# The gates' scratch layout in DRAM: by single first keys, or by groups of four

## The chip, the cores and the metric

One core of a Trainium2 chip runs the whole program. The metric is device time in microseconds (us) of one execution, the median over three runs. PE is the matrix engine and PEld its weight load, DVE the vector engine, ACT the scalar engine, POOL the general engine, SP the engine that only issues transfers. A "q" behind a name (SPq, ACTq) marks an instruction of that engine's sequencer, here the issue of a transfer.

## The reference

A transformer block over 512 tokens of width 1024: two attention mixers, an output projection, and then a PEER layer, which is what the change touches. Cut to its core:

```
q = (hf @ w_q).reshape(T, 8, 2, 128)
scores = einsum('thpd,hpnd->thpn', q, sub_keys)     # two key sets of 128 for each of 8 heads
s, idx = top_k(scores, 16)
cand = s[:, :, 0, :, None] + s[:, :, 1, None, :]    # 16 x 16 pairs
best, pos = top_k(cand, 16)
expert = take(idx0 * 128 + idx1, pos)               # 16384 experts: first key x second key
gate = softmax(best)
y[t] = sum over the 8 * 16 chosen: gelu(hf[t] . u[expert]) * gate * v[expert]
```

## The kernel before

Of the 512 tokens, 128 are served by gathering the rows of u and v that they chose (an indirect transfer on POOL's queue, line 1019, and two DVE passes over each gathered row; spread over the whole second half of the program). The other 384 are computed densely: for each of the 128 first keys e, PE multiplies the 128 experts (e, second key) with all 384 tokens ("up"), ACT applies Gelu, DVE multiplies the result with the gates of these experts (`weigh`), most of them zero, and PE multiplies it with v's 128 rows of e and adds into PSUM over all e ("down"). Matrices are split into a high and a low part (whi and wlo, vhi and vlo, chi and clo), ACT making the high and DVE the low one, and each product is three matmuls.

The gates must therefore be brought into a dense form: a tile of 128 second keys (partitions) by 384 tokens for every first key. That is done in two stages with a scratch tensor `gd` in DRAM between them.

**Writing stage, about 636 to 932 us.** Eight tokens at a time, `onehot` (DVE) makes one-hot matrices of the first and the second key, `spread` (PE, then ACT into `gs`) multiplies them, and when 32 tokens are together one transfer, issued by ACT (line 1191), writes `gs` (128 second keys x 128 first keys x 32 tokens, 2 MB) to `gd`. There are 12 such blocks; the last is written in 4 parts of 512 KB. `gs` has two buffers. Meanwhile `fill` lets PE do "up" products: `some` takes them a 24th at a time, `split_hi` (ACT, line 236) and `split_lo` (DVE) split u's matrix, `up_out` applies Gelu (ACT, line 964) and writes the result to `gad` by a transfer that ACT issues too (line 966). The order of instructions on each engine is fixed when the program is written: an engine runs its list in order, and issuing a transfer is an instruction in that list.

**Reading stage, about 940 to 1615 us.** For each first key in the order `order`: `down(n)`, and behind it on the other engines the work for keys two to four ahead. Keys come in groups of EG = 4; `g_load` (line 1288) reads one group's gates, 128 second keys x 12 blocks x 4 keys x 32 tokens, 768 KB, into `gt` (two buffers), as soon as `weigh` has used up the group two before. 30 of the 32 loads are issued by SP, the first two by POOL. SP's queue also carries v's rows (`vraw`, line 1269), the kept results (`ga`, read from `gad`, line 1316) and u's matrices (`raw`, line 223), in the order in which the program names them.

In `gd` before, one partition's row holds, for each block of 32 tokens, 128 first keys x 32 tokens. A write is 128 runs of 16 KB (in the last block 4 KB), a read of four keys is 128 x 12 runs of 4 x 32 x 4 bytes = 512 B.

Of the kernel before, what the change touches and what calls it, by code (L numbers as in the profile page):

```python
# [10 lines left out]
F32 = mybir.dt.float32  # L11
# [12 lines left out]
T = 512  # L24
# [27 lines left out]
GT = 128  # L52
# [141 lines left out]
def body(ctx, tc, a, out):  # L194
    nc = tc.nc
    pe, act, dve, pool, sp = (Metered(nc.tensor, _pe_ns), nc.scalar, Metered(nc.vector, _dve_ns), nc.gpsimd, nc.sync)
    ctx.enter_context(tc.manual_schedule())
    sb = ctx.enter_context(tc.tile_pool(name="sb", bufs=1))
    dr = ctx.enter_context(tc.tile_pool(name="dr", bufs=1, space=DRAM))
# [11 lines left out]
    queue, raws, ready = [], {}, {}  # L211
# [103 lines left out]
    def pmm(name="pmm"):  # L315
        return ps.tile([128, T], F32, name=name, bufs=4 if name == "pmm" else 2)
# [5 lines left out]
    def tmp(dt=F32, n=T):  # L322
        return tp[0].tile([128, n], dt, name="tmp", bufs=tp[1])
# [80 lines left out]
    def proj(key, xs=None, bank="pmm"):  # L404
        w = weights(key)
        p = pmm(bank)
        acc(p if key[0] != "u" else p[:, GT:], pairs(w, NC_D), xs or hx)
        if key[0] != "u":
            further(key)
        return p  # L410
# [74 lines left out]
    for c in range(NC_D):  # L485
# [28 lines left out]
        if c >= 3 and c - 3 < NT:  # L514
            tt = c - 3
            p = pmm("pst")
# [18 lines left out]
    for i in range(2):  # L535
        p = proj(("w1", 6 + i))
# [14 lines left out]
    for i in range(4):  # L551
        p = proj(("w1", 8 + i))
        t = tmp()
# [68 lines left out]
    for g in range(3):  # L622
        w = weights(("wq", g))
        for i in range(2):
            p = pmm()
# [9 lines left out]
            else:  # L635

                t, x = tmp(), tmp()
# [7 lines left out]
    for i in range(4):  # L645
        p = pmm()
# [5 lines left out]
        if i % 2 == 0:  # L652
            x = turned[i // 2]
# [7 lines left out]
    for tt in range(NT):  # L661
        ts = slice(tt * 128, (tt + 1) * 128)
        p = pmm()
# [142 lines left out]
    for mt in range(8):  # L806
        g = []
        for s in range(2):
            i = 2 * mt + s
            if i in EARLY:  # L810
                t = gin.pop(i)
            else:
                p = proj(("w1", 12 + i))
                t = tmp()
# [6 lines left out]
        for s, y in ((1, yb), (0, ya)):  # L821
            p = pmm()
# [11 lines left out]
    for mt in range(8):  # L834
        p = proj(("wo", mt), mgx)
# [132 lines left out]
    for mt in range(16):  # L968
# [3 lines left out]
        p = proj(("wpq", mt), h2x)  # L972
# [77 lines left out]
    NS = PH * TOPK  # L1050
    i1T, i2T, gh, gl = [pr.tile([128, ND], F16, name=n) for n in ("i1T", "i2T", "gh", "gl")]
    TB = 32
    gd = dr.tile([128, T // TB, 128, TB], F32, name="gd")
    GS = 2.0 ** 15
    def route(tt):
        s4 = srt[:, tt].rearrange("p (h s) k -> p h s k", s=2)
# [115 lines left out]
    def spread(o):  # L1172

        tb, k = divmod(o, SPT)
        if k == 0:
            gst[tb] = pr.tile([128, 128, TB], F32, name="gs", bufs=2)
        gs = gst[tb]
        e1, eh, el = hot.pop(o)
        for q in range(2):
            p = ps.tile([128, 4, 128], F32, name="pst" if q else "pk", bufs=2)  # L1180
            for i in range(4):
                g, t = 2 * q + i // 2, i % 2
                pe.matmul(p[:, i], eh[:, g, :, t], e1[:, g, :, t], start=True, stop=False)
                pe.matmul(p[:, i], el[:, g, :, t], e1[:, g, :, t], start=False, stop=True)
            act.activation(gs[:, :, 8 * k + 4 * q:8 * k + 4 * q + 4], p.rearrange("p t i -> p i t"), AF.Copy,
                           scale=1.0 / GS)
        if k == SPT - 1:
            parts = 4 if tb == T // TB - 1 else 1
            n = 128 // parts
            for i in range(parts):  # L1190
                act.dma_start(gd[:, tb, i * n:(i + 1) * n].rearrange("p i t -> p (i t)"),
                              gs[:, i * n:(i + 1) * n].rearrange("p i t -> p (i t)"))

    up_out()
    split_hi()
# [22 lines left out]
    for o in range(O0, NO + 1):  # L1218
        if o < NO:
            if o == O0 or o % 16 == 0:  # L1220
                for _ in rt or ():
                    fill()
                rt = route(o // 16 + 1) if o // 16 + 1 < NT else None
                rate = 24.0 / (min(16, 16 - o % 16) - 1)
            onehot(o)
            fill()
            due += rate
            while due >= 1.0:
                due -= 1.0
                if rt and next(rt, 1):  # L1230
                    rt = None
                fill()
        if o > O0:
            spread(o - 1)
        gathered(GO)
        fill()
# [1 line left out]


    dn = ax.enter_context(tc.tile_pool(name="dn", bufs=1))  # L1240
    EG = 4
    NG = 128 // EG
    NTB = ND // TB
    NBK = ND // 128
    ga = {}
    vst, vraw, gts, cs = {}, {}, {}, {}


    rest = -(128 - left[0] + LEAVE) % EG
    NB[0] = 128 - left[0] + LEAVE + rest  # L1250
    left[0] = LEAVE + rest
    kept, fresh = list(range(NB[0] // EG)), list(range(NB[0] // EG, NG))
    seq = []
    nk, nf = len(kept), len(fresh)
    while kept or fresh:
        x = kept if not fresh or len(kept) * nf >= len(fresh) * nk and kept else fresh
        seq.append(x.pop(0))
    order = [EG * g + j for g in seq for j in range(EG)]
    kept = [e for e in order if e < NB[0]]
# [25 lines left out]
    def g_load(n, queue=sp):  # L1285
        if n < NG:
            gts[n] = dn.tile([128, NTB, EG, TB], F32, name="gt", bufs=2)
            queue.dma_start(gts[n], gd[:, GT // TB:, seq[n] * EG:(seq[n] + 1) * EG, :])

    def weigh(n):  # L1290
        if n < 128:
            e = order[n]
            x3 = ga[e].rearrange("p (b t) -> p b t", t=TB)
            dve.tensor_tensor(x3, x3, gts[n // EG][:, :, n % EG], op=OP.mult)
            if n % EG == EG - 1:
                g_load(n // EG + 2)
# [58 lines left out]
    for _ in range(VB):  # L1355
        v_load(pool)
    g_load(0, pool)
    refill(pool)
    g_load(1, pool)
    trail(LEAVE + rest - BEFORE - 2)  # L1360
    for n in range(3):
# [99 lines left out]
```

## Time and profile before

| | |
|---|---|
| median of 3 runs | 1637.24 us (1635.01 to 1640.02) |
| the profiled execution | 1637.02 us, of which the span of its instructions is 1635.2 us |
| granted PE clock over the span | 0.998 of full speed |
| PE busy | 98% of the span |
| DVE, ACT, POOL busy | 76%, 44%, 22% |
| moved by DMA | 415.82 MB in 154610 packets, 254 GB/s on average |

Times in the profile count from the first instruction. A matmul's shown duration overlaps its neighbours', so PE's busy share says that something was in flight and not that PE went at its full rate; the rate is seen from the starts of successive matmuls. An issue's duration on SPq or ACTq is the time that the sequencer spent on it, and the transfer lands later.

### The profile page before, as it was taken

The numbers are of one execution on the slowest core, as the hardware profiler recorded it, in microseconds if no ns is written. First come the engines' busy times: TensorE is split into PE (matmuls) and PEld (weight loads), VectorE is DVE, ScalarE is ACT, GpSimd is POOL, SyncE is SP. The second block draws the span as 40 slices with busy tenths as digits, with TensorE's granted clock in tenths as the row PEclk, the third lists the DMA queues.
The fourth block names the chain that finished last, engine by engine and source line by source line (L and its number), as shares of the span: only waits on it lengthen the run. The fifth ranks groups of instructions, "written<-read, shape, count | busy, mean of one in ns | idle before, by whom it ended". The sixth has DMA issues, their size and how long they took to land.

```text
span 1635.2 us, 23193 instructions
## 1 busy us (share of the span) xinstructions
PE 1603.7 (98%) x8487; PEld 1393.1 (85%) x8487; DVE 1240.3 (76%) x2517; ACT 726.0 (44%) x1252; POOL 355.6 (22%) x258
## 2 busy tenths in 40 slices
PE   7999999999999999999999999999999999999998
PEld 6777657888889999999999999888888888888876
DVE  6635665253897989889989747778988888988885
ACT  5453544243333646456455544344443443444343
POOL 4342243445354100000001111111211111111110
PEclk9999999999999999999999999999999999999999
DMA  5222122443333777788789898999999999999994
GB/s 172 64 89 78 52 71 91 169 146 110 125 115 111 233 264 279 261 311 296 266 311 348 330 345 296 318 361 347 392 383 350 386 365 370 367 344 361 364 379 152
DMA packets 154610, 415.82 MB, mean 254 GB/s; under 512 B 12343, under 2 KB 87608, under 8 KB 136448
## 3 DMA queue, kind: packets, MB, share of 16 engines
q1 hardware_dynamic: 118048, 230.28, 40.2%
q0 software_dynamic: 19888, 139.23, 22.2%
q10 hardware_dynamic: 16560, 44.83, 7.3%
q8 instruction: 66, 1.08, 0.3%
q14 instruction: 48, 0.39, 0.1%
HBM read 361.60 MB, written 52.17 MB: 253 GB/s over the span
## 4 chain that ended last, share of the span: by engine, by line
PE 83%; DMA 4%; DVE 4%; issue 4%; ACT 1%; POOL 1%; SPq 0%; DVEq 0%; POOLq 0%; ACTq 0%
PE pmm L161 61%; PE pst L161 11%; PE pk L161 10%; DMA ga<-gad 2%; DMA vraw<-in_v 1%; DVE vlo L161 1%; POOL wlo L242 1%; DMA raw<-in_u 1%; DVE rows L161 1%; DVE rB L161 0%; DVE gout L161 0%; ACT whi L236 0%; DVE tmp L161 0%; DVE clo L161 0%; DVE t L161 0%
## 5 line engine op out<-in xcount | busy, mean ns | idle before, releaser
L161 PE MATMUL pmm<-act_hi,whi 128*128 128x384 f32 (+1 forms) x1016 | 361.8, 356 | 9.4 <-ACT act_hi L331 9.0
L161 PE MATMUL pmm<-act_hi,wlo 128*128 128x384 f32 (+1 forms) x1016 | 353.5, 348 | 3.7 <-DVE wlo L161 2.0
L161 PE MATMUL pmm<-act_lo,whi 128*128 128x384 f32 (+1 forms) x1016 | 353.2, 348 | 0.5 <-DVE act_lo L161 0.5
L1019 POOL DMA_INDIRECT rows<-in_uv,gidx x128 | 130.8, 1022 | 890.5 <-DVE gout L161 846.7
L236 ACT ACTIVATE whi<-raw 128x1024 fp32r<-128x1024 f32 (+1 forms) x201 | 209.2, 1042 | 94.8 <-PE pmm L161 50.9
L242 POOL TENSOR_TENSOR wlo<-raw,whi 128x1024 fp32r<-128x1024 f32 (+1 forms) x79 | 186.2, 2361 | 250.2 <-ACT whi L236 211.5
L161 DVE TENSOR_TENSOR wlo<-raw,whi 128x1024 fp32r<-128x1024 f32 x122 | 148.9, 1223 | 91.4 <-ACT whi L236 89.8
L161 PEld LDWEIGHTS pmm<-act_hi,whi 128*128 128x128 f32 x1016 | 191.8, 189 | 23.8 <-ACT act_hi L331 9.0
L161 PEld LDWEIGHTS pmm<-act_hi,wlo 128*128 128x128 f32 x1016 | 191.6, 189 | 13.9 <-DVE wlo L161 2.6
L161 PE MATMUL pmm<-vlo,chi 128*128 128x512 f32 x512 | 200.5, 392 | 1.6 <-DVE vlo L161 1.3
L161 PE MATMUL pmm<-vhi,chi 128*128 128x512 f32 x512 | 199.6, 390 | 0.9 <-ACT vhi L1275 0.9
L161 PEld LDWEIGHTS pmm<-act_lo,whi 128*128 128x128 f32 x1016 | 192.0, 189 | 8.7 <-DVE act_lo L161 1.0
L161 PE MATMUL pmm<-vhi,clo 128*128 128x512 f32 x512 | 199.3, 389 | 0.0
L161 DVE SCALAR_TENSOR_TENSOR gout<-rows,gact,gout 128x1024 f32<-128x1024 f32 x128 | 164.4, 1284 | 0.0
L161 DVE TENSOR_TENSOR vlo<-vraw,vhi 128x1024 fp32r<-128x1024 f32 x128 | 156.4, 1222 | 4.7 <-ACT vhi L1275 4.7
L1275 ACT ACTIVATE vhi<-vraw 128x1024 fp32r<-128x1024 f32 x128 | 134.0, 1049 | 50.5 <-DMA vraw<-in_v 50.0
L161 DVE SCALAR_TENSOR_TENSOR rows<-rows,hrep 128x1024 f32<-128x1024 f32 x128 | 156.2, 1221 | 0.0
L161 PE MATMUL pmm<-t,whi 128*128 128x512 f32 x436 | 137.7, 397 | 0.0
L161 PEld LDWEIGHTS pmm<-vlo,chi 128*128 128x128 f32 x512 | 96.1, 188 | 25.7 <-DVE vlo L161 6.0
L1031 ACT ACTIVATE gact<-gact 128x1 f32<-128x1 f32 x128 | 25.8, 202 | 205.8 <-DVE rows L161 205.6
L161 PEld LDWEIGHTS pmm<-vhi,chi 128*128 128x128 f32 x512 | 96.1, 188 | 19.9 <-ACT vhi L1275 1.3
L161 PEld LDWEIGHTS pmm<-vhi,clo 128*128 128x128 f32 x512 | 96.1, 188 | 19.0
(276 smaller groups left out, 2775.3 us busy)
## 6 DMA issues: line engine op xcount, KB each, us to landing
raw<-in_u SPq DMA_DIRECT2D x128, 512.0 KB, 5.5
vraw<-in_v SPq DMA_DIRECT2D x124, 512.0 KB, 8.5
gt<-gd SPq DMA_DIRECT2D x30, 768.0 KB, 10.4
gd<-gs ACTq DMA_DIRECT2D x11, 2048.0 KB, 8.2
gad<-gx ACTq DMA_DIRECT2D x96, 192.0 KB, 5.0
ga<-gad SPq DMA_DIRECT2D x95, 192.0 KB, 9.6
raw<-in_w SPq DMA_DIRECT2D x28, 512.0 KB, 3.3
raw<-in_wpq SPq DMA_DIRECT2D x16, 512.0 KB, 3.5
```

What stands on the lines that cost most here:

```text
L161: return f(*args, **kw)
L236: act.activation(hi[:, :n], raw[:, :n], AF.Copy)
L242: (lo_eng or lo_home[0]).tensor_tensor(lo[:, :n], raw[:, :n], hi[:, :n], op=OP.subtract)
L1019: pool.indirect_dma_start(out=rows[n], out_offset=None, in_=a["uv"], in_offset=bass.IndirectOffsetOnAxis(ap=gidx[:, n:n + 1], axis=0))
L1031: act.activation(g, g, AF.Gelu)
L1275: act.activation(hi, vraw[n], AF.Copy)
```

## The change

The scratch tensor `gd` gets the shape [32 groups, 128 second keys, 16 blocks, 4 keys x 32 tokens] in place of [128 second keys, 16 blocks, 128 first keys, 32 tokens]. A group's gates of one second key then lie together: a read takes 128 runs of 12 x 512 B = 6 KB. A write of one block puts 128 x 32 runs of 512 B, whose places in one partition's list are one group (1 MB) apart. The tiles in the core's own memory, the number of transfers, their issuing engines, their order and their bytes stay as they are.

```
-    gd = dr.tile([128, T // TB, 128, TB], F32, name="gd")
+    EG = 4
+    gd = dr.tile([128 // EG, 128, T // TB, EG * TB], F32, name="gd")
...
             parts = 4 if tb == T // TB - 1 else 1
             n = 128 // parts
             for i in range(parts):
-                act.dma_start(gd[:, tb, i * n:(i + 1) * n].rearrange("p i t -> p (i t)"),
-                              gs[:, i * n:(i + 1) * n].rearrange("p i t -> p (i t)"))
+                act.dma_start(gd[i * n // EG:(i + 1) * n // EG, :, tb].rearrange("g p x -> p g x"),
+                              gs[:, i * n:(i + 1) * n].rearrange("p (g j) t -> p g (j t)", j=EG))
...
-    EG = 4
     NG = 128 // EG
...
             gts[n] = dn.tile([128, NTB, EG, TB], F32, name="gt", bufs=2)
-            queue.dma_start(gts[n], gd[:, GT // TB:, seq[n] * EG:(seq[n] + 1) * EG, :])
+            queue.dma_start(gts[n], gd[seq[n], :, GT // TB:].rearrange("p b (j t) -> p b j t", j=EG))
```

## Rows read from the trace of the kernel before

**Rows 1.** The page's line of engine busy time, share of the span, instructions.
```profile
PE 1603.7 (98%) x8487; PEld 1393.1 (85%) x8487; DVE 1240.3 (76%) x2517; ACT 726.0 (44%) x1252; POOL 355.6 (22%) x258
```
**Rows 2.** Busy time by stage: length, engines, clock, DMA share, GB/s.
```profile
640.00:930.00 290.00, 290.00 (x2125) 283.46 (x2122) 259.86 (x487) 151.44 (x264) 21.48 (x21) 1.00 0.83 301
1000.00:1500.00 500.00, 499.94 (x2338) 429.97 (x2337) 421.05 (x558) 211.26 (x404) 81.73 (x81) 1.00 0.97 360
```
**Rows 3.** Chain that ended last, reading stage: start, length, what.
```profile
960.06 11.31 DMA raw<-in_u
...
986.23 2.72 PE pmm L161 x12
988.95 1.37 PE pst L161 x6
990.32 8.32 PE pk L161 x48
...
1502.01 16.70 DMA ga<-gad
...
1540.86 13.85 DMA vraw<-in_v
...
1614.71 3.57 PE pmm L161 x32
```
**Rows 4.** SP's issues in order of time: start, length, transfer.
```profile
958.97 0.38 SPq L1288 DMA_DIRECT2D gt<-gd  x1
960.06 5.77 SPq L223 DMA_DIRECT2D raw<-in_u  x3
...
1120.10 0.38 SPq L1288 DMA_DIRECT2D gt<-gd  x1
1121.70 3.47 SPq L1269 DMA_DIRECT2D vraw<-in_v  x1
...
1539.26 0.37 SPq L1288 DMA_DIRECT2D gt<-gd  x1
...
1599.34 3.98 SPq L1417 DMA_DIRECT2D raw<-x2d  x3
1603.42 1.42 SPq L1269 DMA_DIRECT2D vraw<-in_v  x1
```
**Rows 5.** DMA view of 1602 to 1604 us: one queue's packets, MB, share.
```profile
q1 hardware_dynamic: 1006, 0.53, 91.9%
```
**Rows 6.** DMA views: ACT's queue in 640 to 930 us; the page's issues.
```profile
q10 hardware_dynamic: 10128, 33.55, 30.7%
...
gd<-gs ACTq DMA_DIRECT2D x11, 2048.0 KB, 8.2
```
**Rows 7.** ACT's instructions in order of time around three writes.
```profile
793.46 0.33 ACTq L1191 DMA_DIRECT2D gd<-gs  x1
...
798.88 0.33 ACTq L966 DMA_DIRECT2D gad<-gx  x1
...
846.95 0.33 ACTq L1191 DMA_DIRECT2D gd<-gs  x1
...
847.85 0.33 ACTq L966 DMA_DIRECT2D gad<-gx  x1
...
850.28 1.04 ACT L236 ACTIVATE whi<-raw 128x1024 fp32r<-128x1024 f32 x1
...
929.99 2.87 ACTq L1191 DMA_DIRECT2D gd<-gs  x4
932.91 1.06 ACT L236 ACTIVATE whi<-raw 128x1024 fp32r<-128x1024 f32 x1 [2.95 <-issue]
```
**Rows 8.** DVE behind it, and DVE's waits of 640 to 930 us.
```profile
851.36 1.23 DVE L161 TENSOR_TENSOR wlo<-raw,whi 128x1024 fp32r<-128x1024 f32 x1 [0.35 <-ACT whi L236]
...
DVE wlo L161 <- ACT whi L236: 23.8, 27, 2.1
```
**Rows 9.** Tile gt, fresh keys: durations in ns min/median/max, first and last start.
```profile
L161 DVE TENSOR_TENSOR gf<-gf,gt x28: 551/558/564, 982.6 to 1554.0; 128x384 f32<-128x384 f32 x28
```

## The prediction

> **What bounds the kernel now.** I read the engine shares first, then the busy time by stage, then the chain of waits, then the issues of the two queues that carry `gd`, and last what stands behind those issues on ACT and DVE. PE is busy for 98% of the span and no other engine over 76% [rows 1]; in the stage that writes `gd` PE is never idle by the profile, at full clock, with DVE at 259.9 of 290 us and DMA at 0.83; in the stage that reads it PE is just as full and DMA stands at 0.97 [rows 2]. So the change moves work from a full DMA to one with some room, in front of a PE that hardly waits.
>
> How much PE can win back is seen from its rhythm. One `down` is 12 + 6 matmuls in 2.72 + 1.37 us, 4.08 us, and an `up` of 24 half of 8.32, 4.16 us [rows 3]. The reading loop runs 126 `down`s before its tail; 28 keys are computed fresh in it [rows 9], two of their `up`s before the first `down`. So 126 x 4.08 + 26 x 4.16 = 622 us of matmuls. The chain begins that loop at 986.23 and leaves it at 1614.71 [rows 3], 628.5 us. **PE loses about 6 us to waits in the whole reading loop**, nearly all late, where the chain goes through transfers of `ga` and `vraw` 12 to 17 us long [rows 3]. At the change of stages it loses some 2 to 3 us more, where the chain hangs on a load of u of 11.31 us at 960.06. Together at most 9 us, 0.55%.
>
> What these transfers have in common is on SP's queue. The load at 960.06 is issued right behind the `gt` load of 958.97, the one at 1540.86 behind that of 1539.26 [rows 3, 4]. The `gt` load of 1536 pieces costs SP only 0.38 us itself, but the next issue then takes 3.47 us (at 1121.70), that is until 5.07 us after the `gt` issue began; three loads of x2d of 1024 pieces of 512 B each (8 runs of 128 tokens in each of 128 partitions) keep the queue from 1599.34 until the next transfer is taken at 1604.84, 5.5 us for 3072 pieces, in a quiet moment [rows 4]. A transfer in many pieces holds whoever issues the next one on that queue.
>
> **The change part by part.**
>
> *Reads.* 32 loads go from 1536 pieces to 128. A 512 B piece costs 29 ns of one DMA engine: 91.9% of 16 engines for 2 us, over 1006 packets [rows 5]. 49152 such pieces are 49152 x 29 / 16 = 90 us. In large pieces the same 25.2 MB costs what ACT's queue pays now, 0.307 x 290 x 16 / 33.55 = 42 us per MB, over 16 engines 67 us [rows 6]. So 23 us of DMA time leave a stage of 640 us, 3.6% of a share of 0.97 [rows 2], and the hold behind each `gt` goes: v's rows, `ga` and u get out up to 3.5 us earlier. Worth between nothing and 9 us; I take 5, since transfers on the chain are just the held ones, but DVE is busy for 421 of 500 us there [rows 2] and will not give all of it back. The two loads issued by POOL get shorter issues, off the path.
>
> *Writes, as DMA work.* The 12 blocks go from 128 pieces each to 4096. They are priced as the reads were, 67 to 90 us, +23 us into 295 us: the DMA share rises from 0.83 to about 0.91, below what the reading stage carries today with PE full [rows 2]. Cost zero by itself.
>
> *Writes, as an issue on ACT.* This is the part that sets my number. SP has nothing else to do, so a hold costs it little; ACT issues the `gd` write in the midst of its computing, and the next transfer on the same queue is a `gad` write, 0.90 us later at 846.95 and 5.42 us later at 793.46 [rows 7]; I take 2 as a middle, nearer to the short end. That a held issue stops ACT's computing is in the trace: the four part writes at 929.99 take 2.87 us, and the split behind them waits 2.95 us for nothing but issue [rows 7]. How long would 4096 pieces hold it? Lower bound: nothing, if ACT's queue takes them without back-pressure. From the x2d loads in quiet, 5.5 x 4096/3072 = 7.3 us; from the `gt` load under full DMA, 5.07 x 4096/1536 = 13.5 us [rows 4]. The DMA here is between these; since a queue need not be empty before it takes the next transfer, I stay near the quiet row: 8 us, a hold of 8 - 2 = 6 us, 11 times.
>
> Queued behind the held `gad` issue on ACT are the evacuations of `gs`, a Gelu and the high split of u's next matrix (850.28), for which DVE's low split already waits (0.35 us at 851.36; 27 such waits in the stage, 23.8 us) [rows 7, 8]. DVE runs in order, so the hold passes to it, and with it to the one-hot matrices that PE needs. Between 847.85 and 850.28 ACT has about 0.7 us to spare. DVE's idle time in the stage is 290 - 259.9 = 30.1 us [rows 2], 2.7 us for each of 11 writes. What is left, 6 - 0.7 - 2.7 = 2.6 us per write, DVE cannot make up, and PE, which takes its inputs from DVE, follows: 11 x 2.6 = 29 us. The lead of some matmuls that PE has over DVE absorbs this once and not each time; I leave it out. The block written in 4 parts already pays 2.87 us and would pay about the 5.5 us of the x2d loads: +2.6, set against the 2 to 3 us that the stage change may win.
>
> *A rule beside this.* DMA: Bandwidth & Descriptors, section Anatomy of one DMA, of the Trainium skill says that many descriptors can be emitted before their cost shows; it says so of the path from GpSimd. By it the hold would be nil and the time the one of the first rival below. SP's rows, 3.47 us behind 1536 pieces, do not agree with it.
>
> **Sum.** 1637.0 (the profiled execution, 0.2 below the median shown) + 29 - 5 = 1661; I say 1660 us.
>
> **The rivals.**
>
> (a) *No hold on ACT, or one that is absorbed; faster.* The write's pieces are taken from ACT as fast as they come, or within the 2 us before the next `gad` write. Then only the reads' gain is left, 5 to 9 us: 1628 to 1632. For it: several issues right behind a `gt` load take the usual third of a microsecond, and ACT is busy for only 151 of 290 us in the stage [rows 2]. Against it: rows 4 and the 2.95 us on ACT. The point that decides is a hold of 0.7 + 2.7 = 3.4 us, a write taken within 5.4 us.
>
> (b) *They cancel.* With a hold of 3.4 to 4.2 us the loss is 0 to 9 us and the gain 5: 1632 to 1642. Or PE's waits in the reading loop stay and the hold is absorbed.
>
> (c) *A write of 512 B pieces costs the DMA itself far more than a read.* No row shows such a write. At 58 ns a piece, twice the read's price, the writes take 178 us in place of 67, the share would be 0.83 + 0.38 = 1.2 of a stage of 290 us, and PE would wait for u: +60 us at least, above 1700. The room is 0.17 x 290 = 49 us, so it decides from (67 + 49) x 16 / 49152 = 38 ns per piece.
> The same page of the Trainium skill, section Latency and other measured facts, has HBM rates that fall with a row pitch of a large power of two, 207 GB/s at 512 KiB and 164 at 2 MiB; consecutive pieces of a partition lie 1 MiB apart here. As an estimate by that page a 2 MB write takes 10 to 13 us. The full writes land after 8.2 us now [rows 6]; no run yet shows the new pitch.
>
> (d) *The layout brings nothing to the reads*, because the 512 B pieces are not what fills the DMA: 3.6% less of it, and the gathers and v's rows stay. Then the 5 us are missing: 1666, within the forecast's own range.
>
> **How the numbers follow.** Under 0.3% (5 us) this kernel's runs cannot be told from no change. Forecast with (d), 1642 to 1700: 0.62. (a) 0.20, (b) 0.13, (c) 0.05. Faster 0.20, same 0.13, slower 0.67. The forecast's own range goes from a hold of 4.2 us (11 x 0.8 = 9, less 5: 1641) to one of 9.6 us (11 x 6.2 = 68, less 5: 1700). The range over all cases is 1629 to 1700.
>
> **What would show it.** Right: ACT issues of `gad` behind a `gd` write that last several us in place of 0.33; ACT waits for issue; DVE's waits on the high split well above 23.8 us; gaps in PE between 640 and 935 us; that stage some 30 us longer. In the reading loop, issues behind `gt` at 0.33 to 0.43 us, and the loop under 628 us. Wrong: `gad` issues that stay at 0.33 us, or a PE that goes on without gaps although ACT is held, because its inputs were made earlier than I reckon.

## The result, and the profile after

The changed kernel takes 1663.36 us (median) against 1637.12 us; the ratio is 1.0156, with a 95% interval of 1.0133 to 1.0179. It is slower, by about 26 us where 23 were forecast. (One execution of 2288 us at a mean clock of 0.653 is left out of the ratio; the others lie between 1660.43 and 1664.58.) The profiled execution has a span of 1662.8 us, 27.6 us more than before, and the times below are from it.

The busy time by stage of the changed kernel, columns as in [rows 2]:

```profile
640.00:930.00 290.00, 275.32 (x1931) 265.50 (x1929) 236.41 (x458) 137.65 (x238) 19.64 (x19) 0.98 0.85 277
...
1000.00:1500.00 500.00, 500.00 (x2369) 434.62 (x2368) 415.22 (x546) 214.03 (x401) 78.57 (x77) 1.00 0.94 356
```

In the writing stage PE now stands still for 14.7 of 290 us, and its mean granted clock is 0.98: with levels of 1.2 and 2.4 GHz that is 4% of the time at the lower one. In the reading stage PE is full, and the DMA share has come down from 0.97 to 0.94.

The instructions on `gs`, first of the kernel before, then of the changed one; the last two times are the first and the last start:

```profile
L1185 ACT ACTIVATE gs<-pst x48: 592/594/634, 612.6 to 929.4; 128x512 f32<-128x512 f32 x48
```
```profile
L1186 ACT ACTIVATE gs<-pst x48: 587/592/607, 612.6 to 959.7; 128x512 f32<-128x512 f32 x48
```

The chain of the changed kernel at the first and behind the last `down` of the reading loop:

```profile
1019.71 2.72 PE pmm L161 x12
...
1642.29 3.57 PE pmm L161 x32
```

From these lines and [rows 3] the program divides into stages. **Writing** (first to last evacuation of `gs`): 316.8 us before, 347.1 after, +30.3. **Change of stages** (from there to the first `down`): 986.23 - 929.4 = 56.8 before, 60.0 after, +3.2. **Reading loop**: 628.5 before, 622.6 after, -5.9. The sum, +27.6, is the whole difference of the spans.

The writing stage ends where ACT does its last evacuation of `gs`, and PE is not at the same place of its own list then. Its busy time and matmuls in the writing stage before, then in the writing stage and the change of stages after, columns as in [rows 2]:

```profile
612.60:929.40 316.80, 316.80 (x2314) 309.63 (x2314) 285.38 (x555) 167.54 (x290) 23.38 (x23) 1.00 0.82 299
```
```profile
612.60:959.70 347.10, 330.22 (x2330) 318.02 (x2330) 285.23 (x561) 167.49 (x290) 23.42 (x23) 0.98 0.83 273
959.70:1019.71 60.01, 54.03 (x297) 53.07 (x296) 24.21 (x26) 23.71 (x35) 8.12 (x13) 0.94 0.91 324
```

In the changed kernel 16 matmuls more lie ahead of this boundary. At the pace of [rows 3], 48 in 8.32 us, they are 2.8 us of work that has moved from one stage into the other. What PE lost is therefore about 27.5 us in the writing stage and 6.0 at the change of stages.

Why the writing stage is longer is seen on ACT. Its issues of more than 0.9 us between 636 and 940 us in the changed kernel, in order of time (start, length), then ACT and DVE around the one at 909.58:

```profile
638.37 4.86 ACTq L966 DMA_DIRECT2D gad<-gx  x1
673.12 6.89 ACTq L966 DMA_DIRECT2D gad<-gx  x1
709.37 5.79 ACTq L966 DMA_DIRECT2D gad<-gx  x1
736.18 7.15 ACTq L966 DMA_DIRECT2D gad<-gx  x1
766.86 7.64 ACTq L966 DMA_DIRECT2D gad<-gx  x1
811.17 1.20 ACTq L966 DMA_DIRECT2D gad<-gx  x1
836.73 6.77 ACTq L966 DMA_DIRECT2D gad<-gx  x1
860.33 9.36 ACTq L966 DMA_DIRECT2D gad<-gx  x1
892.66 3.44 ACTq L966 DMA_DIRECT2D gad<-gx  x1
909.58 9.94 ACTq L966 DMA_DIRECT2D gad<-gx  x1
937.80 7.80 ACTq L966 DMA_DIRECT2D gad<-gx  x1
```
```profile
907.69 0.38 ACTq L1192 DMA_DIRECT2D gd<-gs  x1
...
909.58 9.94 ACTq L966 DMA_DIRECT2D gad<-gx  x1
919.57 0.60 ACT L1186 ACTIVATE gs<-pk 128x512 f32<-128x512 f32 x1 [10.02 <-PE pst L161]
```
```profile
922.05 1.23 DVE L161 TENSOR_TENSOR wlo<-raw,whi 128x1024 fp32r<-128x1024 f32 x1 [7.78 <-ACT whi L236]
```

The `gd` write itself costs ACT 0.38 us; the harmless little `gad` write behind it holds ACT for 9.94 us, and DVE then waits 7.78 us for its high split. Note the bracket on ACT's line: the idle time is put down to PE, which released the evacuation long before; the issue in the line above is what filled it. There is one such hold for each of the 11 full writes, 70.8 us in all.

PE at the end of that chain, its instructions of the changed kernel with an idle time before them (905 to 930 us), and DVE's waits of 640 to 930 us as in [rows 8]:

```profile
922.07 0.45 PE L161 MATMUL pmm<-act_hi,whi 128*128 128x384 f32 x1 [1.67 <-ACT whi L236]
...
925.87 0.29 PE L161 MATMUL pk<-x,xh 128*128 128x128 f16 x1 [2.09 <-DVE x L161]
```
```profile
DVE wlo L161 <- ACT whi L236: 51.3, 16, 7.8
```

On SP the opposite has happened. The issues around one `gt` load of the changed kernel:

```profile
1550.10 0.32 SPq L1288 DMA_DIRECT2D gt<-gd  x1
1551.71 0.33 SPq L1269 DMA_DIRECT2D vraw<-in_v  x1
1552.09 0.42 SPq L1316 DMA_DIRECT2D ga<-gad  x1
```

The load behind it is taken in 0.33 us, and so is the one behind each of SP's 30 `gt` loads. Before, 16 of the 30 were followed by an issue of 0.9 us or more, among them the 3.47 us in [rows 4] and this one:

```profile
1540.86 3.62 SPq L1269 DMA_DIRECT2D vraw<-in_v  x1
```

### The profile page after: what moved, and what is told of

Its sections match the earlier page's. It is cut to its first block, busy times and chain, and to the rows that moved or that the text cites. A ratio compares the mean times of both kernels' runs of the same rounds, so it can differ in the third digit from the quotient of the medians.

```text
span 1662.8 us, 23193 instructions
## 1 busy us (share of the span) xinstructions
PE 1613.0 (97%) x8487; PEld 1401.7 (84%) x8487; DVE 1239.6 (75%) x2517; ACT 728.2 (44%) x1252; POOL 354.9 (21%) x258
## 4 chain that ended last, share of the span: by engine, by line
PE 78%; DVE 5%; ACTq 4%; issue 4%; ACT 3%; DMA 1%; POOL 1%; SPq 0%; DVEq 0%; POOLq 0%
PE pmm L161 56%; PE pst L161 12%; PE pk L161 10%; ACTq L966 4%; DVE wlo L161 1%; ACT gs L1186 1%; ACT whi L236 1%; DMA ga<-gad 1%; POOL wlo L242 1%; DVE rows L161 1%; DVE x L161 1%; ACT gx L964 0%; ACTq L1192 0%; DMA vraw<-in_v 0%; DVE rB L161 0%
## 5 line engine op out<-in xcount | busy, mean ns | idle before, releaser
L161 PE MATMUL pmm<-act_hi,wlo 128*128 128x384 f32 (+1 forms) x1016 | 357.2, 352 | 13.2 <-DVE wlo L161 11.4
L1019 POOL DMA_INDIRECT rows<-in_uv,gidx x128 | 131.0, 1024 | 904.5 <-DVE gout L161 862.9
## 6 DMA issues: line engine op xcount, KB each, us to landing
gd<-gs ACTq DMA_DIRECT2D x11, 2048.0 KB, 14.2
```

The source lines that it names most:

```text
L161: return f(*args, **kw)
L1019: pool.indirect_dma_start(out=rows[n], out_offset=None, in_=a["uv"], in_offset=bass.IndirectOffsetOnAxis(ap=gidx[:, n:n + 1], axis=0))
```

## The experiments

All ratios are to the kernel before in runs on the same chip; its median beside the first four experiments (reads only to quarters) was 1638.44 us, and beside the others 1636.59. The stages are read from each trace in the way shown above (expectations that count the writing stage from the first to the end of the last evacuation have 0.6 us more). They come from one profile of each kernel: with the same reads, the loop differs by up to 1.6 us from kernel to kernel.

| kernel | median, us | ratio to before, 95% | writing | change | loop |
|---|---|---|---|---|---|
| before | 1637.12 | | 316.8 | 56.8 | 628.5 |
| changed | 1663.36 | 1.0156, 1.0133 to 1.0179 | 347.1 | 60.0 | 622.6 |
| reads only | 1631.07 | 0.9947, 0.9927 to 0.9966 | 316.8 | 54.9 | 622.6 |
| writes only | 1677.20 | 1.0222, 1.0178 to 1.0265 | 351.2 | 60.4 | 630.5 |
| `gad` from SP | 1636.73 | 0.9988, 0.9970 to 1.0005 | 316.7 | 58.8 | 622.6 |
| quarters | 1639.11 | 0.9994, 0.9978 to 1.0011 | 316.7 | 60.1 | 624.2 |
| halves | 1642.73 | 1.0038, 1.0022 to 1.0055 | 322.1 | 59.5 | 623.6 |
| `gd` from POOL | 1638.23 | 1.0014, 0.9996 to 1.0031 | 316.8 | 62.5 | 623.1 |
| quarters, last block by SP | 1634.98 | 0.9983, 0.9964 to 1.0003 | 316.7 | 58.8 | 622.7 |
| quarters, last block plain | 1634.77 | 0.9985, 0.9973 to 0.9997 | 316.7 | 57.1 | 624.7 |

**Reads only.** On the kernel before:

```
-            queue.dma_start(gts[n], gd[:, GT // TB:, seq[n] * EG:(seq[n] + 1) * EG, :])
+            w = NTB * EG * TB
+            flat = gd[:, GT // TB:].rearrange("p b i t -> p (b i t)")
+            queue.dma_start(gts[n].rearrange("p b j t -> p (b j t)"), flat[:, seq[n] * w:(seq[n] + 1) * w])
```

> The reads' part of the change alone: the scratch tensor is written as before (128 runs of 16 KB a block, by ACT), and each of the 32 loads reads 128 runs of 6 KB out of it, every byte once. The gates that reach a key are then other ones than the reference's; times, sizes and order of all instructions stay. Theory (the reads win what PE loses in the reading loop, the writes cost the rest): issues of gad stay at 0.33 us, the writing stage stays as it was before, the reading loop shrinks from 628.5 to about 622.5 us, total 1628 to 1632, ratio to before 0.995 to 0.997. Rival (the reads win nothing, the loop got shorter in the changed kernel only because its writing stage was slow and left less to catch up): loop 627 to 629 us, ratio 0.999 to 1.001.

Measured 1631.07 us, ratio 0.9947, as the theory has it: the writing stage is what it was, the loop is 622.6 us. The first and last lines of its chain's loop:

```profile
986.22 2.72 PE pmm L161 x12
...
1608.80 3.57 PE pmm L161 x32
```

The loop starts at the very time of the kernel before and ends 5.9 us earlier. So the reads' gain is real by itself and owes nothing to a slow writing stage; the rival falls. (This kernel leaves out that each key gets its own gates; its result is another one.) Whether the gain comes from the hold on SP that is gone or from the DMA work that is saved, no run here separates.

**Writes only.** On the changed kernel:

```
-    gd = dr.tile([128 // EG, 128, T // TB, EG * TB], F32, name="gd")
+    gd = dr.tile([128, T // TB, 128 // EG, 2, EG * TB], F32, name="gd")
-                act.dma_start(gd[i * n // EG:(i + 1) * n // EG, :, tb].rearrange("g p x -> p g x"),
+                act.dma_start(gd[:, tb, i * n // EG:(i + 1) * n // EG, 0],
-            queue.dma_start(gts[n], gd[seq[n], :, GT // TB:].rearrange("p b (j t) -> p b j t", j=EG))
+            queue.dma_start(gts[n], gd[:, GT // TB:, seq[n], 0].rearrange("p b (j t) -> p b j t", j=EG))
```

> The writes' part alone, without the 1 MB distance: each partition's row of the scratch tensor holds, for a block of 32 tokens, 32 groups of 512 B, 1 KB apart; a write is 4096 runs of 512 B near each other, a load is 1536 runs of 512 B as before the change. Theory (the hold on ACT comes from the number of pieces): gad issues behind a write of 5 to 10 us, the writing stage about 30 us longer, total 1665 to 1675, ratio 1.017 to 1.023, full writes landing after 12 to 16 us as in the changed kernel. Rival (the 1 MB distance in DRAM is what makes the write slow and so holds ACT): writes land after 9 to 10 us, holds under 4 us, ratio 1.000 to 1.008.

Measured 1677.2 us, ratio 1.0222; the median is 2 us above the range. The issues of `gad` in this kernel, 630 to 960 us, minimum, median and maximum in ns:

```profile
L966 ACTq DMA_DIRECT2D gad<-gx x61: 326/327/10334, 630.1 to 956.7; - x61
```

With pieces 1 KB apart ACT is held for as long as 10.3 us, against 9.94 us with pieces 1 MB apart, and the writing stage is no shorter (351.2 against 347.1 us). The distance in DRAM is not the cause. The reading loop, with its reads as before the change, takes 630.5 us and has none of the gain. This trace has no landing times, so that part of the expectation can't be read.

**`gad` from SP.** On the changed kernel:

```
-                act.dma_start(gad[e], g)
+                sp.dma_start(gad[e], g)
```

> The changed kernel, but the writes of gad are issued by SP; ACT still issues the gd writes of 4096 pieces. Theory (only the next transfer on the same queue is held): ACT's next issue is the next gd write some 24 us later, so ACT is not held; the writing stage is as long as before the change, total 1629 to 1637, ratio 0.995 to 1.000. Rival 1 (the small pieces crowd the DMA engines and u's loads come late): writing stage still 20 to 30 us longer, ratio 1.010 to 1.016. Rival 2 (SP, which now has to wait for each Gelu before it goes on to u's loads, becomes late itself): waits of ACT for raw loads, ratio 1.005 to 1.02.

Measured 1636.73 us, ratio 0.9988; the writing stage is back at 316.7 us although every `gd` write still goes out from ACT in 4096 pieces. ACT, then SP, around one write of this kernel; then ACT's queue in the DMA view of 640 to 930 us, and the busy time of that stretch:

```profile
849.74 0.37 ACTq L1192 DMA_DIRECT2D gd<-gs  x1
850.15 0.49 ACT L964 ACTIVATE gx<-pmm 128x384 f32<-128x384 f32 x1 [0.44 <-ACT gs L1186]
851.18 0.60 ACT L1186 ACTIVATE gs<-pk 128x512 f32<-128x512 f32 x1 [0.53 <-PE pk L161]
```
```profile
850.67 0.33 SPq L966 DMA_DIRECT2D gad<-gx  x1
```
```profile
q10 hardware_dynamic: 45232, 23.07, 28.5%
```
```profile
640.00:930.00 290.00, 290.00 (x2119) 283.46 (x2118) 262.02 (x494) 148.60 (x261) 21.53 (x21) 1.00 0.91 303
```

This run decides between hold and crowding. The pieces are all there, the DMA share is 0.91, even above the 0.85 of the changed kernel, and PE is never idle. ACT's queue carries `gd` alone here, so it gives the price of a small write: 0.285 x 290 x 16 us over 45232 packets, 29 ns, the same as a small read [rows 5]. Both rivals fall.

**Quarters.** On the changed kernel, where `late` is emptied by one at the end of each spread:

```
+        if late:
+            late.pop(0)()
         if k == SPT - 1:
-            parts = 4 if tb == T // TB - 1 else 1
+            last = tb == T // TB - 1
+            parts = 4
...
+            for i in range(parts):
+                if last or i == 0:
+                    put(i)
+                else:
+                    late.append(lambda i=i: put(i))
```

> The changed kernel, but each of the 11 full blocks is written in 4 transfers of 1024 pieces, the first at the block's end and the others each one spread (8 tokens) later; all on ACT, same bytes and pieces. Theory (a transfer is taken when most of the previous one's pieces are out, so the hold depends on the pieces of one transfer): 1024 pieces are out before or soon after the next gad issue 0.9 to 2 us later, holds under 1.5 us each, covered by DVE's idle time; total 1630 to 1640, ratio 0.995 to 1.002. Rival (the hold goes with all pieces sent, however they are divided, since the queue passes them at a fixed rate): the sum of the issue times stays near 75 us, ratio 1.010 to 1.017.

Measured 1639.11 us, ratio 0.9994; writing stage 316.7 us. The `gad` issues of 630 to 960 us:

```profile
L966 ACTq DMA_DIRECT2D gad<-gx x68: 326/326/942, 634.5 to 955.2; - x68
```

The same pieces in transfers of 1024 hold the next `gad` issue for at most 0.94 us. The hold is not a fixed toll per piece; the rival falls.

**Halves.** The same with two transfers for a block (`parts = 4 if last else 2`).

> The changed kernel, each full block written by ACT in 2 transfers of 2048 pieces, the second one spread (8 tokens) later. Theory (the hold follows the pieces of one transfer; 4096 are taken after 8.8 us on average in the changed kernel, 1024 are hardly felt in the quarters): 2048 are taken after some 4 us, so gad issues behind them last 2 to 3.5 us, below the 3.4 us that I reckoned DVE's idle time to cover; the writing stage (first to last evacuation of gs) 317 to 323 us against 317.4 before and 347.7 in the changed kernel, total 1634 to 1642. Rival (what counts is the sum of holds over a block, not each one): the sum stays above 40 us and the stage takes 335 us or more, total above 1650.

Measured 1642.73 us, ratio 1.0038, 0.7 us above the range; writing stage 322.1 us. ACT's issues above 3.4 us in the second part of the stage:

```profile
831.69 4.94 ACTq L966 DMA_DIRECT2D gad<-gx  x1
...
848.28 5.06 ACTq L966 DMA_DIRECT2D gad<-gx  x1
...
897.76 6.24 ACTq L966 DMA_DIRECT2D gad<-gx  x1
...
915.45 4.80 ACTq L966 DMA_DIRECT2D gad<-gx  x1
```

Holds were longer than I expected, up to 6.24 us, and those above 0.6 us add up to 63 us, not far below the changed kernel's 75 by the same count. Yet the stage grew by 5.3 us and not by 30. So it is not the sum that counts. What lies above the cover of 3.4 us that the prediction reckoned is 1.5 + 1.7 + 2.8 + 1.4 = 7.4 us here, and 35.6 us over the eleven holds of the changed kernel; the stages grew by 5.3 and 30.3 us. PE's part in the 5.3 us is smaller still, by its busy time in the halves' writing stage:

```profile
612.40:934.50 322.10, 320.07 (x2330) 312.42 (x2330) 285.43 (x555) 167.12 (x290) 23.36 (x23) 1.00 0.88 294
```

It stands still for 2.0 us, and 2.8 of the 5.3 us are again the 16 matmuls that lie ahead of the boundary.

**`gd` from POOL.** `act.dma_start(gd...` becomes `pool.dma_start(gd...` in the changed kernel.

> The changed kernel, but all gd writes are issued by POOL, whose other work in this stage is one gather issue per 11 us or so. Theory (ACT must not be the one behind the write): ACT's issues stay at 0.33 us, writing stage 317 to 319 us, total 1629 to 1640. Rival (POOL needs several us to make 4096 pieces, and stands behind gathers that wait up to 18 us, so that the gs buffers come free late and ACT waits for them): writing stage over 325 us, total above 1645.

Measured 1638.23 us, ratio 1.0014. The writing stage is back at 316.8 us and POOL needs 1.74 us for a write of 4096 pieces; but the change of stages takes 62.5 us, the longest of all (PE stands still for 5.4 us in it, at a mean granted clock of 0.95), and that eats the loop's gain. POOL's issues:

```profile
L1192 POOL DMA_DIRECT2D gd<-gs x15: 895/1743/1759, 638.6 to 934.8; - x15
```

**The last block.** Two more on the quarters: the last block's four transfers issued by SP (`put(i, sp)`); or the last block in a tensor of its own in the old layout, read by a second transfer for each group:

```
+    gz = dr.tile([128, 128, TB], F32, name="gz")
...
+                    act.dma_start(gz[:, i * n:(i + 1) * n].rearrange("p i t -> p (i t)"),
+                                  gs[:, i * n:(i + 1) * n].rearrange("p i t -> p (i t)"))
...
+            queue.dma_start(gts[n][:, :NTB - 1], gd[seq[n], :, GT // TB:T // TB - 1].rearrange("p b (j t) -> p b j t", j=EG))
+            queue.dma_start(gts[n][:, NTB - 1], gz[:, seq[n] * EG:(seq[n] + 1) * EG])
```

> The quarters, with the last block's four transfers issued by SP. In the quarters ACT is still held 4.8 us there (2.9 before the change), and the stretch from the last evacuation of gs to the first product of the reading loop is 59.5 us against 56.2 before and 54.3 with the reads' part alone. Theory A (the hold on ACT at the last block costs these us): the stretch falls to 55 to 57 us, total 1632 to 1636. Theory B (the last block's 4096 pieces land later, and v's first loads, which take over the memory of gs, wait for that): the stretch stays at 58 us or more, total 1636 to 1641.

> The quarters, with the last block in a scratch tensor of its own in the old layout (4 writes of 128 runs of 4 KB); each group is then read by two transfers, 128 runs of 5.5 KB and 128 runs of 512 B. Theory (the layout's gain in the reading loop without a hold anywhere and without a late last block): stage 317 us, stretch to the loop 54 to 56 us, loop 622.6 us as in the changed kernel, total 1629 to 1634, ratio to before 0.994 to 0.997, the best version. Rival (32 more transfers on SP's queue and their 512 B pieces cost what the reads won): loop 625 us or more, total 1635 or more.

Measured 1634.98 us (ratio 0.9983, change of stages 58.8 us) and 1634.77 us (0.9985, interval 0.9973 to 0.9997; change 57.1 us, loop 624.7 us). Taking the last four issues from ACT wins 1.3 us of 60.1, so most of what the last block costs is not ACT's hold; with the block in large pieces 3.0 us come back. PE and its clock in the change of stages, with the reads alone, in the quarters and with the plain last block:

```profile
931.30:986.22 54.92, 54.32 (x313) 53.91 (x312) 24.36 (x26) 23.70 (x35) 7.89 (x13) 1.00 0.93 357
```
```profile
933.90:994.01 60.11, 55.87 (x313) 55.56 (x312) 24.22 (x26) 23.86 (x35) 8.15 (x13) 0.97 0.93 335
```
```profile
930.40:987.47 57.07, 54.60 (x313) 53.96 (x312) 24.05 (x26) 23.74 (x35) 9.29 (x15) 1.00 0.96 355
```

PE stands still for 0.6, 4.2 and 2.5 us. In the quarters its clock is 0.97 as well, so 6% of these 60 us, right behind PE's longest wait, went by at 1.2 GHz and cost some 2 us. Waits and clock together give the differences of the three lengths to within half a microsecond. With the plain last block the loop is 2.1 us above 622.6; that this is due to the second transfers is not shown, since the quarters, which have none, took 624.2. Both expectations are half met: theory B for the first, and for the second a total 0.8 us above its range. Each version is faster than the changed kernel by 28 us; the second is faster than the kernel before too, by 0.15%, which is at the edge of what can be told. The 7.4 us that the reads alone win were not reached by a kernel that computes the reference.

## Why the prediction was right

- **PE's loss in the reading loop, about 6 us.** Right: the changed loop is 622.6 us, the 622 us of matmuls alone. I took 5 of a possible 9 us; 5.9 came, although DVE is as busy as I feared. Which of the two things that I named gives it, the hold gone or 23 us less DMA work, is not shown. The reads' part alone is 7.4 us faster in the medians (1638.44 in its own comparison).
- **The change of stages.** I set a gain of 2 to 3 us against +2.6 from the last block, so about nothing. It came out at -1.9 with the reads alone and at +3.2 in the changed kernel, 6.0 with the 2.8 us of work that moved across the boundary. The gain is there, as far as one profile shows it; the loss is larger than I put in. It shows as waits of PE (6.0 us in the changed kernel, 2.0 before, 0.6 with the reads alone) and as a clock of 0.94, which the sum did not have. With the clock gone and the last block in large pieces, 2.5 us of waits are left in the last experiment. Why the low split that PE waits for is late there is not shown.
- **The writes as DMA work, nothing by itself.** Right: with `gad` on SP the DMA share is 0.91, the forecast number, at 29 ns a piece, and PE does not wait. Rival (c), a dear small write, is excluded. The pitch rule beside it (the Trainium skill, DMA: Bandwidth & Descriptors, Latency and other measured facts) is about the pitch from one partition's row to the next. I had put the 1 MB between the pieces of one partition in its place. From partition to partition the rows lie 8 KB apart in the changed kernel, so the rule does not bear on it. The full writes do land later, after 14.2 us in place of 8.2. But pieces 1 KB apart hold ACT as long as pieces 1 MB apart, and ACT's queue takes 36.8% of 640 to 930 us with them and 34.8% in the changed kernel, for 31 MB each time.
- **The hold on ACT, 6 us eleven times.** Right in kind and size: 70.8 us, 6.4 us each. The next issue is through 8.8 us after the write's own on average, where I took 8, and begins 2.3 us after it, where I took 2. That the next transfer on the same queue is the one held is shown by moving that one, and that the pieces of one transfer matter by the quarters and halves.
- **The cover of 3.4 us, and luck.** The sum made of it, 11 x 2.6 = 29 us, met the stage's 30.3 us, and in part by luck. Of the 30.3 us, 2.8 are the matmuls that moved across the boundary, and up to 7 are the lower clock (next point), so the waits behind the holds cost 20 us or a little more; PE stands still for 16.9 us by the profile. The eleven holds lie 35.6 us above the 3.4, so the cover was in truth larger than I reckoned. The halves say the same: 7.4 us above the cover, and PE stands still for 2.0. PE's lead over DVE, which I left out, may be what is missing; no run shows it. A cover that was too small and a clock that was left out made up for each other.
- **Not foreseen: the clock.** In the changed kernel's writing stage the granted clock is 0.98, where PE now stands still again and again and before ran without a gap at 1.00; 4% of 347 us at 1.2 GHz are 14 us, which cost up to half of that, 7 us. At the change of stages it is 0.94, around a wait of PE of 5.0 us. Both are part of the measured loss and hide in a sum that I had made without them.
- **The rule on emitting descriptors** (the Trainium skill, DMA: Bandwidth & Descriptors, Anatomy of one DMA) would have had rival (a). POOL, whose path it speaks of, indeed issues 4096 pieces in 1.74 us, and no hold is seen in the writing stage: there the trace agrees. ACT's queue does not behave so, with up to 9.94 us.

## What to carry to other kernels

On the queues of SP and ACT here, the price of a transfer in many small pieces falls on whoever issues the next transfer on the same queue: on SP that delays loads, on an engine that computes it stops the computing. So when pieces must be small on one side of a scratch tensor, put them on the side, and on the queue, whose next issue can wait, or divide the transfer so that each part is out before the next issue comes. And weigh a hold against the idle time of the engine that waits for the held one: in this case many holds of under 1 us cost the stage nothing, and eleven of 6.4 us on average most of 30 us. A wait that stops PE can cost once more by the clock, so look at the granted clock beside the idle time.

## What the runs showed of the hardware

- A piece of 512 B costs 29 ns of one DMA engine, as a read and as a write, 57 us per MB against 42 for large ones, with 1 MB between the pieces as well.
- The next issue behind a transfer of 4096 pieces on ACT's queue took 3.9 to 10.3 us where it came 0.9 to 1.9 us behind it (in the changed kernel and with the writes only), and 1.2 to 3.4 us where it came 6.4 to 6.9 us behind. Behind 2048 pieces it took up to 6.24 us. Behind 1024 a `gad` issue took at most 1.23 us in the three kernels with quarters; in the last block, whose four transfers go out one right behind the other, an issue took up to 2.3 us. The holding transfer's own issue shows nothing of it (0.38 us).
- The same 4096 pieces issued by POOL took it 1.74 us each time.
- The writing stage took 316.7 or 316.8 us in seven kernels, with a DMA share of 0.83 in the kernel before and of 0.91 with `gad` from SP; PE is never idle in either, so PE sets the stage's length there.
- PE's granted clock, 1.00 in the change of stages of the kernel before, was 0.97 in the quarters, where PE had stood still for 4.2 us, and 0.94 in the changed kernel, where it had stood still for 5.0 us at a stretch.
